# Low parts of projection weights by a negated copy and an adding transfer

## The chip, the cores and the metric

The kernel runs on one core of one Trainium2 chip. The metric is device time in microseconds of one execution. The engines: TensorE (PE) multiplies matrices, VectorE (DVE) and ScalarE (ACT) work elementwise on SBUF and PSUM, GpSimd (POOL) is a fourth, programmable engine, SyncE (SP) issues transfers. Sixteen DMA engines carry all transfers. A transfer can be put on the queue of SP, ACT or POOL.

## The reference

A two-layer decoder trunk over 1024 tokens of width 1024, in float32. Each layer:

```
h = rmsnorm(x, attn_norm)
proj = h @ w_in                # 1024 x 1952, split among four token mixers
y_a = latent attention (4 heads, rotary key)      y_b = gated convolution
y_c = pooling over 2/4/8/16 positions             y_d = windowed attention with sinks
mixed = per-group rmsnorm of (y_a, y_b, y_c, y_d)
x = x + mixed @ w_o
x = x + (silu(gate) * up) @ w_down,  gate, up = split(rmsnorm(x) @ w_gate_up)
```

After both layers comes a last rmsnorm.

## The kernel before

Every large product is made of three products of rounded halves. A float32 operand is split into a high part, rounded to the matmul's float32r format, and a low part, what is left. `mm3` adds high x high, high x low and low x high in PSUM; for the weights W and activations R the order is (Wh, Rh), (Wh, Rl), (Wl, Rh), so that the low part of the weights is wanted by the third matmul of each group. One matmul takes 128 x 128 weights and 128 x 512 activations. The feed-forward products go through a seven-product scheme on 2 x 2 blocks (the names B11, N1, T3 and so on).

Weights come from memory as float32 and are split on the chip. `weights` (L206 to L220) does it for one block: SP loads the raw block, ScalarE writes the high part (L218), VectorE subtracts it from the raw block and writes the low part (L219). Blocks wider than 256 columns take raw, high and low tiles from a pool of 47 tile places of 128 x 1024 (`slots`); narrower ones have buffers of their own (vraw, vhi, vlo). `weights_slots` (L256) does the same for two blocks of 128 x 1024 of the output projection in each layer, L266 and L267. `first_blocks` splits the first three projection blocks of layer 0 by another helper, `split` (L286, L287). `rope_weights` (L222) splits its block at L231 and L232.

So `weights` with wide tiles handles, over both layers, 27 blocks of 1024 columns of w_in and 16 blocks of 768 columns of w_o; with narrow tiles 22 blocks. `expect_layer` lists the wide blocks in the order of their use and `ahead` fetches the next one. Every one-block `project` makes two products of 24 matmuls, one for each half of the tokens; its result is evicted by VectorE (L360, L488). Every output block makes two products of 18 matmuls (`out_part`), evicted at L1087. `ring` holds two blocks' high and low tiles; places that come free go to the end of the queue of free places.

The order of the work is not the program's. `order_engines` reads all instructions, and `arrange` simulates the engines with a table of durations and gives each engine's queue a fixed order by readiness and rank. MOVED is a list of shifts of the ranks, some 3,700 entries. The instructions of each engine, SP's transfers too, are then issued in that fixed order. For a transfer on GpSimd's queue the table has this line, which no instruction of the kernel before uses:

```
            if eng == "POOL":
                v.ns, v.tail = 700, 4200
```

that is, 700 ns in the queue and 4200 ns more until it has landed. GpSimd's queue holds 32 memsets of attention (L1045, zeros in the last block of a tile in `mix_values`), two products at the very end (L433) and four at the start.

Of the kernel before, what the change touches and what calls it, by code (L numbers as in the profile page):

```python
# [14 lines left out]
AF = mybir.ActivationFunctionType  # L15
ALU = mybir.AluOpType
AX = mybir.AxisListType

P = 128
# [96 lines left out]
def trunk_kernel(ctx: ExitStack, tc: tile.TileContext, ins, out):  # L116
    nc = tc.nc
    act, dve, pe, pool, sp = nc.scalar, nc.vector, nc.tensor, nc.gpsimd, nc.sync
# [11 lines left out]
    def rd(ap):  # L130
        return ap.bitcast(F32)
# [74 lines left out]
    def weights(src, n):  # L206
        if n > 2 * P:
            s = F.pair()
            raw = F.ap2(s)
            sp.dma_start(raw[:, :n], src)  # L210
            hi, lo = (R.ap2(i) for i in ring_next())
            F.free_pair(s)
        else:
            raw = wpool.tile([P, 2 * P], F32, name="vraw", tag="vraw")
            sp.dma_start(raw[:, :n], src)
            hi = wpool.tile([P, 2 * P], F32R, name="vhi", tag="vhi")
            lo = wpool.tile([P, 2 * P], F32R, name="vlo", tag="vlo")
        act.copy(hi[:, :n], raw[:, :n])  # L218
        dve.tensor_tensor(out=lo[:, :n], in0=raw[:, :n], in1=rd(hi[:, :n]), op=ALU.subtract)  # L219
        return hi, lo  # L220

# [36 lines left out]
    def weights_slots(src, m, n):  # L258

        s = F.pair()  # L260
        raw = F.ap2(s)
# [5 lines left out]
        dve.tensor_tensor(out=lo, in0=raw[:, : m * n], in1=rd(hi), op=ALU.subtract)  # L267
# [178 lines left out]
    for l in range(L):  # L446
# [313 lines left out]
        for ct in range(2):  # L760
# [18 lines left out]
            else:  # L779
# [7 lines left out]
                out=dst,  # L787
# [1765 lines left out]
```

## Time and profile before

| What | Value |
|---|---|
| time, median of 3 runs | 2052.42 us (2051.62 to 2052.92) |
| profiled execution, span | 2050.3 us |
| what lies around the span (median less span) | 2.1 us |
| TensorE busy | 2034.3 us |
| VectorE busy | 1599.7 us |
| ScalarE busy | 981.9 us |
| GpSimd busy | 7.9 us |

For the profiled execution only its span is recorded, so the median of the runs stands in for its own time. The span is cut into 40 slices of 51 us in the profile's second part. Layer 0's projections run up to about 190 us, its latent attention and output projection to about 400, its feed-forward part to about 1000; layer 1 then repeats this. Matmuls overlap each other: one lasts about 390 ns in the rows and the next starts 227 ns after it, so that "busy" alone doesn't show whether they follow each other as closely as they can. In the rows of waits the columns are the total in us, how many there were, and the longest one. In the groups the columns are busy time and mean duration in ns, then the idle time before them and what ended it. In the rows of time the columns are start, length, engine, line, operation and shapes.

### The profile page before, as it was taken

How to read it: one execution, taken by the hardware profiler on the slowest of the kernel's cores; microseconds unless marked ns; L12 is line 12 of the kernel's file. 1: busy time of each engine (PE TensorE's matmuls, PEld its weight loads, DVE VectorE, ACT ScalarE, POOL GpSimd, SP SyncE). 2: the span in 40 equal slices, each digit the busy share in tenths (PEclk: the TensorE clock that was granted, in tenths of full speed). 3: DMA queues.
4: the chain of work that ended last, by engine and by line, in shares of the span. 5: the costliest groups of instructions: out<-in, count | busy, mean ns of one | idle time of the engine just before them, and what ended most of it. 6: DMA issues, size and time to landing. Idle time of an engine off the chain costs nothing. (4 is left out here: it accounts for less than half of the span.)

```text
span 2050.3 us, 26022 instructions
## 1 busy us (share of the span) xinstructions
PE 2034.3 (99%) x9418; PEld 1675.7 (82%) x9418; DVE 1599.7 (78%) x2742; ACT 981.9 (48%) x1713; POOL 7.9 (0%) x38
## 2 busy tenths in 40 slices
PE   9999999999999999999999999999999999999997
PEld 7887888888878888888888878877888888888887
DVE  7889988998778887556566898889987877876555
ACT  6447666653333335344443576657433333354342
POOL 0000000000000000000000000000000000000000
PEclk9999999999999999999999999999999999999999
DMA  5020223355445547766411102142564544487552
GB/s 182 24 73 21 74 84 111 113 190 176 161 143 186 172 154 232 240 236 221 139 37 44 47 22 93 57 146 101 175 203 151 179 160 146 167 295 242 172 195 86
DMA packets 149249, 289.74 MB, mean 141 GB/s; under 512 B 12672, under 2 KB 72064, under 8 KB 149120
## 3 DMA queue, kind: packets, MB, share of 16 engines
q1 hardware_dynamic: 148976, 288.03, 41.8%
q8 instruction: 74, 1.21, 0.2%
q14 instruction: 55, 0.45, 0.1%
q10 hardware_dynamic: 144, 0.05, 0.0%
HBM read 204.67 MB, written 83.36 MB: 140 GB/s over the span
## 5 line engine op out<-in xcount | busy, mean ns | idle before, releaser
L275 PE MATMUL ps_mm<-u,u 128*128 128x512 f32 (+1 forms) x3376 | 858.6, 389 | 0.3 <-DVE u L287 0.2
L275 PEld LDWEIGHTS ps_mm<-u,u 128*128 128x128 f32 x3376 | 617.0, 188 | 130.0 <-issue 5.9
L275 PE MATMUL ps_s<-u,u 128*128 128x512 f32 x2666 | 686.0, 390 | 2.4 <-DVE u L287 2.3
L275 PEld LDWEIGHTS ps_s<-u,u 128*128 128x128 f32 x2666 | 499.4, 188 | 109.6 <-DVE u L287 3.2
L286 ACT CAST u<-u 128x1024 fp32r<-128x1024 f32 (+2 forms) x385 | 334.7, 891 | 451.9 <-PE ps_mm L275 92.5
L287 DVE TENSOR_TENSOR u<-u,u 128x1024 fp32r<-128x1024 f32 (+2 forms) x385 | 387.6, 1023 | 161.3 <-ACT u L286 134.6
L275 PE MATMUL ps_t<-u,u 128*128 128x512 f32 (+1 forms) x1122 | 287.5, 379 | 1.0 <-DVE u L1642 1.0
L275 PEld LDWEIGHTS ps_t<-u,u 128*128 128x128 f32 x1122 | 203.5, 188 | 42.6 <-issue 1.7
L275 PE MATMUL ps_pv<-u,u 128*128 128x512 f32 x744 | 214.7, 390 | 0.5 <-ACT u L286 0.5
L275 PEld LDWEIGHTS ps_pv<-u,u 128*128 128x128 f32 x744 | 139.4, 188 | 30.4 <-ACT u L286 0.9
L289 ACT ACTIVATE u<-u,par 128x512 fp32r<-128x512 f32 x100 | 69.0, 717 | 40.5 <-DVE u L360 14.0
L1394 ACT ACTIVATE tp<-tp 128x512 f32<-128x512 f32 x84 | 52.8, 631 | 71.5 <-DVE tp L360 71.4
L164 DVE TENSOR_TENSOR u<-u 128x256 f32<-128x256 f32 x176 | 73.4, 421 | 14.9 <-DMA u<-in_w_dn 12.7
L286 ACT CAST u<-ps_t 128x512 fp32r<-128x512 f32 (+3 forms) x128 | 60.9, 501 | 50.2 <-PE ps_t L1036 28.0
L287 DVE TENSOR_TENSOR u<-ps_t,u 128x512 fp32r<-128x512 f32 (+3 forms) x128 | 71.7, 576 | 13.9 <-ACT u L286 12.7
L1262 ACT COPY tn<-ps_s 128x512 f32<-128x512 f32 x64 | 37.4, 584 | 79.5 <-PE ps_s L275 77.3
L290 DVE SCALAR_TENSOR_TENSOR u<-u,par,u 128x512 fp32r<-128x512 f32 x100 | 72.5, 746 | 3.1 <-ACT u L289 3.0
L321 ACT ACTIVATE tn<-u 128x512 f32<-128x512 f32 (+1 forms) x93 | 52.9, 592 | 35.4 <-DVE u L1642 25.7
L1395 DVE TENSOR_TENSOR tp<-tp,u 128x512 f32<-128x512 f32 x84 | 57.2, 686 | 11.8 <-ACT tp L1394 11.6
L219 DVE TENSOR_TENSOR u<-u,u 128x1024 fp32r<-128x1024 f32 (+1 forms) x43 | 48.1, 1119 | 16.0 <-PE ps_mm L275 6.4
L218 ACT CAST u<-u 128x1024 fp32r<-128x1024 f32 (+1 forms) x43 | 41.8, 971 | 39.0 <-DMA u<-in_w_in 26.7
L360 DVE TENSOR_TENSOR tp<-tp,u 128x512 f32<-128x512 f32 x84 | 57.3, 685 | 0.5
(196 smaller groups left out, 2007.3 us busy)
## 6 DMA issues: line engine op xcount, KB each, us to landing
u<-in_w_gu SPq DMA_DIRECT2D x88, 512.0 KB, 3.9
ad<-u SPq DMA_DIRECT2D x154, 256.0 KB, 2.1
u<-ad SPq DMA_DIRECT2D x70, 512.0 KB, 5.0
u<-in_w_dn SPq DMA_DIRECT2D x68, 512.0 KB, 3.7
qd<-u SPq DMA_DIRECT2D x44, 512.0 KB, 3.2
u<-qd SPq DMA_DIRECT2D x32, 512.0 KB, 5.2
u<-in_w_in SPq DMA_DIRECT2D x27, 512.0 KB, 3.5
u<-in_xT SPq DMA_DIRECT2D x32, 256.0 KB, 5.0
```

What stands on the lines that cost most here:

```text
L164: dve.tensor_tensor(out=o, in0=o, in1=u, op=ALU.add)
L218: act.copy(hi[:, :n], raw[:, :n])
L219: dve.tensor_tensor(out=lo[:, :n], in0=raw[:, :n], in1=rd(hi[:, :n]), op=ALU.subtract)
L275: pe.matmul(o, w, r, start=start and k == 0 and i == 0, stop=stop and k == n - 1 and i == 2, skip_group_check=again,)
L286: act.copy(hi, f)
L287: dve.tensor_tensor(out=lo, in0=f, in1=rd(hi), op=ALU.subtract)
L289: act.activation(hi, f, AF.Copy, scale=gain)
L290: dve.scalar_tensor_tensor(out=lo, in0=f, scalar=gain, in1=rd(hi), op0=ALU.mult, op1=ALU.subtract)
L321: act.activation(q, f, AF.Square)
L360: dve.tensor_tensor(out=o, in0=a, in1=b, op=ALU.mult)
L1394: last_silu = act.activation(g, g, AF.Silu)
L1395: dve.tensor_tensor(out=g, in0=g, in1=r, op=ALU.mult)
```

## The change

For the 47 wide blocks (43 in `weights`, 4 in `weights_slots`) the subtraction on VectorE is gone. ScalarE, after it has written the high part, writes the raw block once more, rounded in the same way and multiplied by -1, into the low tile. A transfer on GpSimd's queue then adds the raw block, read as float32, onto the low tile. What stands in the low tile is again raw less rounded. The 22 narrow blocks, `first_blocks` and `rope_weights` are as before. The list MOVED is replaced by another one (3,776 entries for 3,708), so the order of all engines' instructions is another one as well; the functions that make the order are the same.

```diff
         act.copy(hi[:, :n], raw[:, :n])
-        dve.tensor_tensor(out=lo[:, :n], in0=raw[:, :n], in1=rd(hi[:, :n]), op=ALU.subtract)
+        if n > 2 * P:
+            rest(lo[:, :n], raw[:, :n])
+        else:
+            dve.tensor_tensor(out=lo[:, :n], in0=raw[:, :n], in1=rd(hi[:, :n]), op=ALU.subtract)
         return hi, lo
+
+    def rest(lo, raw):
+
+        act.activation(lo, raw, AF.Copy, scale=-1.0)
+        pool.dma_start(rd(lo), raw, accum_op=ALU.add)
...
         act.copy(hi, raw[:, : m * n])
-        dve.tensor_tensor(out=lo, in0=raw[:, : m * n], in1=rd(hi), op=ALU.subtract)
+        rest(lo, raw[:, : m * n])
         return h, l
...
 MOVED = """
...
 """
```

704 rows, old and new, of the table MOVED are left out of this document.

## The prediction

> **What bounds the kernel now.** I read the page first: engine shares and the slices.
>
> ```profile
> span 2050.3 us, 26022 instructions
> PE 2034.3 (99%) x9418; PEld 1675.7 (82%) x9418; DVE 1599.7 (78%) x2742; ACT 981.9 (48%) x1713; POOL 7.9 (0%) x38
> PE   9999999999999999999999999999999999999997
> DVE  7889988998778887556566898889987877876555
> PE 27%; DVE 0%; ACT 0%; issue 0%; DVEq 0%
> ```
>
> TensorE is busy in all 40 slices but the last, and the chain that ended last is nearly all TensorE. VectorE, which the change relieves, is 78% busy and has two humps: slices 3 to 9 and 23 to 29. A busy TensorE could still hide short stalls, so I compare its pace. Then the stages:
>
> ```profile
> 1825.55 22.44 PE ps_s L275 x99
> ...
> 0.00:25.00 25.00, 23.83 (x101) 19.33 (x102) 19.46 (x35) 20.20 (x32) 0.20 (x4) 1.00 0.88 320
> 25.00:190.00 165.00, 165.00 (x805) 135.85 (x804) 134.57 (x294) 92.50 (x204) 0.00 (x0) 1.00 0.13 43
> 190.00:350.00 160.00, 159.17 (x807) 129.97 (x805) 141.57 (x306) 105.70 (x245) 3.26 (x16) 1.00 0.23 75
> ...
> 450.00:1000.00 550.00, 548.28 (x2419) 453.47 (x2418) 407.50 (x587) 219.03 (x292) 0.00 (x0) 1.00 0.57 192
> 1000.00:1200.00 200.00, 200.00 (x960) 164.70 (x959) 139.16 (x296) 93.42 (x203) 0.00 (x0) 1.00 0.15 48
> 1200.00:1350.00 150.00, 149.51 (x751) 121.53 (x750) 133.48 (x290) 98.66 (x228) 2.65 (x14) 1.00 0.21 69
> 2000.00:2050.00 50.00, 39.86 (x296) 37.37 (x294) 28.20 (x57) 14.42 (x33) 1.41 (x2) 0.94 0.24 85
> ```
>
> Columns: window, length, busy time of TensorE, its weight loads, VectorE, ScalarE, GpSimd, granted clock, DMA share, GB/s. In the chain 99 matmuls take 22.44 us, 226.7 ns each; 2419 of them make 548.4 us of the 550 in the feed-forward stage, so that stage runs at the matmul's own pace. TensorE's idle time is 16.0 us over the span: 10.1 in the last 50 us, 1.2 in the first 25, 1.7 in the feed-forward, and 1.3 in the two stages 190 to 350 and 1200 to 1350, where the layers' attention runs and VectorE is 88% and 89% busy (141.57/160, 133.48/150). The changed weights are made between 25 and 350 and between 990 and 1360. The waits say what little TensorE waited for:
>
> ```profile
> PE ps_s L275 <- DVE u L287: 2.3, 2, 1.7
> PE ps_mm L275 <- DVE u L913: 1.3, 4, 0.6
> PE ps_mm L275 <- DVE u L287: 0.2, 1, 0.2
> ...
> PEld ps_s L275 <- DVE u L287: 3.2, 2, 2.2
> PEld ps_t L1036 <- DVE u L287: 2.2, 10, 0.3
> PEld ps_mm L275 <- DVE u L287: 0.9, 2, 0.7
> PEld ps_pv L1048 <- DVE u L287: 0.9, 5, 0.2
> PEld ps_mm L848 <- DVE u L360: 0.7, 2, 0.4
> PEld ps_mm L275 <- DVE u L219: 0.6, 2, 0.4
> ```
>
> TensorE's matmuls waited 3.8 us for VectorE (first three rows), its weight loads at least 8.5 us (the last six, which contain the first three's stalls in part). For the subtraction that goes away, L219, weight loads waited 0.6 us.
>
> **The change, part by part.** Prices:
>
> ```profile
> L219 DVE TENSOR_TENSOR u<-u,u 128x1024 fp32r<-128x1024 f32 x27 | 32.9, 1220 | 15.2 <-PE ps_mm L275 6.4 <-PE ps_pv L340 3.7 <-PE ps_t L275 2.9
> L219 DVE TENSOR_TENSOR u<-u,u 128x768 fp32r<-128x768 f32 x16 | 15.2, 950 | 0.7 <-ACT u L218 0.6
> L267 DVE TENSOR_TENSOR u<-u,u 128x1024 fp32r<-128x1024 f32 x4 | 4.9, 1221 | 0.8 <-ACT u L266 0.8
> L728 ACT ACTIVATE u<-u,par 128x1024 f32<-128x1024 f32 x4 | 4.6, 1144 | 3.5 <-DVE u L360 3.5
> L1021 ACT ACTIVATE u<-u,sm 128x512 f32<-128x512 f32 x16 | 10.9, 721 | 1.6 <-DVE sm L1016 1.6
> ...
> qd<-u SPq DMA_DIRECT2D x44, 512.0 KB, 3.2
> u<-qd SPq DMA_DIRECT2D x32, 512.0 KB, 5.2
> ```
>
> Removed: 47 subtractions, 32.9 + 15.2 + 4.9 = 53.0 us of VectorE, which falls to 1546.7 us (75%). The 22 narrow blocks and the first three blocks of layer 0 keep theirs.
>
> Added on ScalarE: 47 scaled copies. A scaled copy of 1024 columns is the L728 row, 1.14 us; 768 columns by the line through L728 and L1021 are 0.93 us. 31 x 1.14 + 16 x 0.93 = 50.3 us; ScalarE goes to 1032 us, 50%. In 190 to 350 it gets some 2 x 1.14 more for the joint blocks, 1.14 for the last projection block and 8 x 0.93, 11 us on 105.7 of 160, 73%: it doesn't become the bound there. Its cover is that idle quarter; without it the 11 us would stand ahead of the splits (L286) that matmuls wait for.
>
> Added on GpSimd's queue: 47 transfers of 512 or 384 KB within the SBUF, in a queue that held only memsets in these stages. The trace has no adding transfer and none issued by GpSimd. Below: the plain 512 KB store, 3.2 us. Above: the addition reads two streams, so twice the plain load, 10.4 us. I take 5, by the single load (5.2) and by what the kernel's own order writer plans (700 ns of issue and 4200 to landing), for which the new order was written. Engines for it are free: DMA shares are 0.13 to 0.23 in these stages; 47 times 3.2 to 10.4 us of all 16 engines is 150 to 490 us beside 2050. Memsets wait behind it for its issue, by the plan 0.7 us: the 32 memsets are hidden as long as a block's other matmuls cover that; without cover at most 20 transfers in attention x 0.7 = 14 us.
>
> What gets later is the low part: before, 1.22 us behind the rounded part, now 1.14 + 5, so 4.9 us later at the same place in the order (2 us at 3.2, 10.3 at 10.4). The raw tile is held as long, and loads that take its place start later. What covers this is the distance from the low part to its first matmul:
>
> ```profile
> 1054.76 1.23 DVE L219 TENSOR_TENSOR u<-u,u 128x1024 fp32r<-128x1024 f32 x1 [2.05 <-PE ps_t L275]
> 1103.13 0.69 DVE L488 SCALAR_TENSOR_TENSOR te<-ps_mm,u 128x512 f32<-128x512 f32 x1 [0.32 <-PE ps_mm L275]
> ...
> 342.10 0.96 DVE L219 TENSOR_TENSOR u<-u,u 128x768 fp32r<-128x768 f32 x1 [0.19 <-ACT u L218]
> 362.78 0.68 DVE L1087 TENSOR_TENSOR u<-u,ps_mm 128x512 f32<-128x512 f32 x1
> ...
> 86.07 1.22 DVE L219 TENSOR_TENSOR u<-u,u 128x1024 fp32r<-128x1024 f32 x1
> 95.94 0.69 DVE L360 TENSOR_TENSOR u<-ps_mm,u 128x512 f32<-128x512 f32 x1 [1.82 <-PE ps_mm L275]
> 260.63 0.95 DVE L219 TENSOR_TENSOR u<-u,u 128x768 fp32r<-128x768 f32 x1
> 267.14 0.69 DVE L1087 TENSOR_TENSOR u<-u,ps_mm 128x512 f32<-128x512 f32 x1 [0.52 <-PE ps_mm L275]
> 1273.24 0.95 DVE L219 TENSOR_TENSOR u<-u,u 128x768 fp32r<-128x768 f32 x1
> 1281.17 0.69 DVE L1087 TENSOR_TENSOR u<-u,ps_mm 128x512 f32<-128x512 f32 x1 [0.82 <-PE ps_mm L275]
> ```
>
> Each pair is a low part and the eviction of its first product, matched by counting both in program order. From an eviction I go back 24 matmuls (5.4 us; 18 and 4.1 for the output projection); where the eviction shows a wait for TensorE it follows the product at once, in the second pair it may stand later, so that its cover is an upper bound. Layer 1's seventh block is ready at 1056.0 and used by 1097.7: 42 us of cover. The last output block of layer 0 has 343.1 to 358.7, 16 us. The shortest: layer 0's fifth streamed block (87.3 to 90.5, 3 us) and the third output block of both layers (261.6 to 263.0, 1.5 us, and 1274.2 to 1277.1, 2.9 us). So 4.9 us more is hidden nearly everywhere by work already ahead; at the three places it would cost 1.9 + 3.4 + 2.0 = 7.3 us if the order stayed. The new order counts on 4.9 us, so I take 0 for it and keep 7.3 for the range.
>
> Two notes from outside the sum. The Trainium skill ("DMA: Bandwidth & Descriptors", Anatomy of one DMA) gives a GpSimd transfer some 2.0 us plus bytes at 436 GB/s, by my estimate 3.2 us for 512 KB without addition; with that the low part would be 3 us later and the second place would cost 1.6 us, the third 0.2; no row of this profile shows such a transfer. Against the change stands "SBUF — State Buffer" (the "DVE blocks DMA" trap): GpSimd can't write its descriptors while VectorE runs an operation that uses both ports. What would do that here are the rescalings of attention:
>
> ```profile
> 78.27 1.15 DVE L609 TENSOR_SCALAR tp<-tp,sm 128x256 f32<-128x256 f32 x4
> ```
>
> Four in a row hold VectorE 1.15 us, so a transfer issued at such a moment lands 1.15 us later.
>
> The sum: VectorE's relief gives back some of the 3.8 us of matmul waits. The removed work lies only partly ahead of them: in 190 to 350 it is about 11 of 141.57 us, which brings that stage from 88% to 81%. I take half, 1.9 us. Late low parts 0, ScalarE 0, memsets 0. 2050.3 - 1.9 = 2048.4 of span. The median of the runs is 2052.42, 2.1 above the span, so 2050.5.
>
> **The rivals.**
>
> More comes back. Beyond the visible gaps lie the weight loads' 8.5 us: if VectorE's humps are what keeps the order tight, the new order can pack TensorE closer there. For: 88 and 89% busy. Against: 10.1 us of the idle time lie at the end, where nothing changes. Up to 8.5, likeliest 7: 2045.
>
> The low parts come late (slower). Place: third output block of each layer and the fifth streamed block. It decides once low parts come more than 1.5 us later than now; at 4.9 us and unmoved matmuls 7.3 us, 2050.5 + 7.3 = 2058. For: third block's raw load ends right ahead of its rounding, so nothing can be made earlier there. Against: 13 us and more of cover elsewhere, and an order that plans for it.
>
> The addition takes 10.4 us. Then low parts are 10.3 us later: 7.3 + 8.8 + 7.4 = 23.5 us at these places, 2074.
>
> GpSimd held up by VectorE's rescalings: 1.15 at each of three places, 3.5 us: 2054. I give it little, since rescalings are 4 in a row at most and the covers are long.
>
> Nothing of VectorE's 53 us was on the path: 2052.4. The change would do what it says and show it only in VectorE's share.
>
> **How the numbers follow.** Forecast (2047 to 2054) 0.42; more comes back 0.28; late low parts 0.14; slow addition 0.07; rescalings 0.03; nothing 0.06. About 0.2%, 4.1 us, is what a measurement can tell from no change: faster is below 2048.3, slower above 2056.5. Faster: 0.28 + 0.06 of the forecast's lower edge = 0.34. Slower: 0.14 + 0.07 + 0.01 = 0.22. The rest, 0.44, is the same. The range takes in 2052.4 - 8.5 and some rounding of it, 2042, and late low parts with half again their price, 2062; outside stay the slow addition and the extremes, about 0.13.
>
> **What would show it.** VectorE near 1547 us and ScalarE near 1032; 47 scaled copies of 0.93 to 1.14 us; 47 transfers of GpSimd landing in about 5 us. TensorE still at 99% with 10 us idle at the end. The forecast is wrong if weight loads wait more than a few us for GpSimd's transfers, above all around 263 and 1277, or if TensorE's idle time in 190 to 350 changes by more than a few us; a landing time above 7 us would point to the late cases.

## The result, and the profile after

The changed kernel takes 2101.07 us (median of 4 runs, 2099.52 to 2107.25), the kernel before beside it 2052.33 (2051.62 to 2052.92): a ratio of 1.0242, 95% interval 1.0227 to 1.0257. It is 48.7 us slower. The profiled execution has a span of 2100.7 us, 50.4 more than before. From the page of the changed kernel:

```profile
span 2100.7 us, 26162 instructions
PE 2054.7 (98%) x9418; PEld 1672.6 (80%) x9418; DVE 1554.9 (74%) x2695; ACT 1021.6 (49%) x1760; POOL 48.2 (2%) x85
PE   9999899999999999999999999999999999999998
DVE  6778786988778777655646897779987687775645
PE 80%; DVE 7%; DMA 7%; ACT 3%; issue 2%; SPq 0%; DVEq 0%; ACTq 0%; POOLq 0%
```

VectorE lost 44.8 us of work and ScalarE gained 39.7, where the prediction had 53.0 and 50.3. TensorE falls below 9 only in slice 5, at about 210 to 260 us, and in the last. The chain that ended last passes through VectorE, transfers and ScalarE for 17% of the span. That can't be set against the zeros of the page before: there the chain could be followed back over the last 27% of the span only. What was added has these prices (groups by shape, then transfers with their size and the median time from issue to landing):

```profile
L227 ACT ACTIVATE u<-u 128x1024 fp32r<-128x1024 f32 x31 | 32.8, 1058 | 12.7 <-DMA u<-in_w_in 5.8 <-DVE sm L368 3.1 <-PE ps_mm L283 2.0
L227 ACT ACTIVATE u<-u 128x768 fp32r<-128x768 f32 x16 | 13.5, 847 | 5.4 <-DMA u<-in_w_o 4.7 <-DVE u L298 0.5
L228 POOL DMA_DIRECT2D u<-u x47 | 40.7, 867 | 1238.1 <-ACT u L227 1131.0 <-ACT u L294 38.7 <-PE ps_s L583 21.6
```

```profile
u<-u POOLq DMA_DIRECT2D x31, 512.0 KB, 4.8
u<-u POOLq DMA_DIRECT2D x16, 384.0 KB, 4.5
```

In the mean nothing costs more than was thought: copies of 1.06 and 0.85 us, transfers that land after 4.8 and 4.5 us (medians; the 47 lie between 3.9 and 7.8). The stages, with the columns of the prediction's table:

```profile
190.00:350.00 160.00, 152.22 (x743) 121.83 (x742) 126.33 (x282) 108.41 (x245) 10.24 (x23) 0.97 0.35 92
450.00:1000.00 550.00, 543.11 (x2372) 443.28 (x2372) 400.74 (x586) 205.79 (x273) 0.00 (x0) 1.00 0.56 187
1000.00:1200.00 200.00, 197.99 (x952) 164.86 (x951) 123.97 (x270) 102.79 (x204) 10.38 (x12) 1.00 0.41 110
1200.00:1350.00 150.00, 146.26 (x701) 116.01 (x699) 122.27 (x255) 102.38 (x216) 8.64 (x18) 1.00 0.31 80
```

In 190 to 350 TensorE issues 743 matmuls where it had issued 807, and in 1200 to 1350 it issues 701 for 751. So far this fits late low parts. The feed-forward row doesn't: 2372 for 2419, though no changed weight and no adding transfer runs there (GpSimd: 0.00). What TensorE's matmuls waited for in the changed kernel (total, times, longest):

```profile
PE ps_s L283 <- DVE te L1585: 6.9, 3, 4.4
PE ps_t L283 <- ACT u L294: 3.8, 3, 2.0
PE ps_s L283 <- DVE u L295: 3.3, 2, 2.8
PE ps_mm L283 <- DMA u<-u: 2.9, 2, 1.9
```

For the adding transfers themselves (`DMA u<-u`) its matmuls waited 2.9 us and its weight loads 3.7. The waits are spread over many lines, most of which the change's code doesn't touch. The changed part that does touch them is the list of shifts, which sets the order of every engine.

### The profile page after: what moved, and what is told of

It reads as the page before. It is cut to its first block, busy times and chain, and to the rows that moved or that the text cites. A ratio compares the mean times of both kernels' runs of the same rounds, so it can differ in the third digit from the quotient of the medians.

```text
span 2100.7 us, 26162 instructions
## 1 busy us (share of the span) xinstructions
PE 2054.7 (98%) x9418; PEld 1672.6 (80%) x9418; DVE 1554.9 (74%) x2695; ACT 1021.6 (49%) x1760; POOL 48.2 (2%) x85
## 4 chain that ended last, share of the span: by engine, by line
PE 80%; DVE 7%; DMA 7%; ACT 3%; issue 2%; SPq 0%; DVEq 0%; ACTq 0%; POOLq 0%
PE ps_mm L283 30%; PE ps_s L283 24%; PE ps_t L283 10%; PE ps_pv L283 7%; DVE u L295 2%; DMA u<-in_w_o 2%; PE ps_pv L1056 1%; PE ps_t L1044 1%; DMA ad<-u 1%; ACT u L294 1%; PE ps_t L353 1%; DMA u<-in_w_in 1%; DMA u<-in_w_dn 1%; DMA u<-in_w_gu 1%; PE ps_s L991 1%
## 5 line engine op out<-in xcount | busy, mean ns | idle before, releaser
L283 PE MATMUL ps_s<-u,u 128*128 128x512 f32 x2666 | 676.5, 392 | 13.3 <-DVE te L1585 6.9
L283 PE MATMUL ps_pv<-u,u 128*128 128x512 f32 x744 | 208.4, 391 | 1.4 <-ACT u L294 1.3
L228 POOL DMA_DIRECT2D u<-u x47 | 40.7, 867 | 1238.1 <-ACT u L227 1131.0
```

The lines of the kernel that those rows point to most:

```text
L228: pool.dma_start(rd(lo), raw, accum_op=ALU.add)
L283: pe.matmul(o, w, r, start=start and k == 0 and i == 0, stop=stop and k == n - 1 and i == 2, skip_group_check=again,)
```

## Experiments: order or transfers

Two theories. "Order": the new issue order is worse on the chip, transfers or not. "Transfers": the later low parts, longer held raw tiles and added traffic cost the time. The first pair crosses the two parts of the change. The issue order of one kernel is written out step by step and given to the other kernel's code:

```diff
-    for queue in arrange(steps).values():
+    for part in np.split(ranks, np.cumsum(ORDER_N)[:-1]):   # ranks: the other kernel's order
+        queue = [steps[r] for r in np.cumsum(part)]
```

The new order with VectorE's subtractions:

> The changed kernel's issue order on every engine, written out step by step, but each of the 47 low parts is again one VectorE subtraction, at the place of the negated copy (or right behind the rounding, where the copy stood ahead of it); no adding transfer runs. Theory 'order' (the new list of shifts gives an order that fits late loads badly; the adding transfers themselves cost little): 2085 to 2105 us, as slow as the change. Rival 'transfers' (the later low parts, the longer held raw tiles or the traffic of the adding transfers delay the loads and TensorE): 2050 to 2062 us.

Measured: 2103.97 us (ratio 1.0247, 1.0229 to 1.0265). Without a single adding transfer the new order is as slow as the change. It is not a pure test, since 53 us of VectorE's work are back in an order that has no room for them.

The old order with the new low parts:

> The kernel before's issue order on every engine, written out step by step; in place of each of the 47 subtractions stands, at the same moment of that order, the negated copy on ScalarE's queue and the adding transfer on GpSimd's. Theory 'order': 2048 to 2062 us (2052.4 plus at most the 7.3 us that late low parts were to cost at three places, less up to 4 for VectorE's relief). Rival 'transfers': 2085 us and more, since every load and low part is delayed as in the changed kernel, with an order that does not plan for it.

Measured: 2146.92 us (1.0458, 1.0442 to 1.0473), 94 us slower than before. Here "order" missed: the adding transfers are very expensive when the order isn't made for them. TensorE's waits in this kernel, the first rows:

```profile
PE ps_mm L285 <- DMA u<-u: 47.7, 14, 6.0
PE ps_mm L285 <- DVE u L923: 5.5, 2, 4.7
PE ps_t L355 <- DVE u L336: 4.9, 3, 1.7
PE ps_s L993 <- ACT u L296: 3.4, 1, 3.4
```

So both parts can cost, each alone. The list of shifts can also be emptied in both kernels:

```diff
-MOVED = """ ... """
+MOVED = ""
```

> The kernel before with an empty list of shifts, so that its order follows the planner's own priorities. Its order writer puts the end at 2067.8 us instead of 2039.9. Both theories: 2075 to 2120 us. It is the pair of after_plain.

> The changed kernel with an empty list of shifts; the order writer puts the end at 2076.3 us, 8.6 more than for before_plain. Theory 'order': within 15 us of before_plain, since neither has a list of shifts. Rival 'transfers': 35 to 60 us more than before_plain, as between the two kernels.

Measured: 2085.48 us (1.0157, 1.0140 to 1.0174) and 2101.83 us (1.0238, 1.0218 to 1.0259). Without lists the new low parts cost 16.4 us, just above the 15 that "order" allowed and far from the 35 to 60 of "transfers". The kernel before gains 33 us from its list. The changed kernel gains nothing measurable from its own (2101.83 without, 2101.07 with), though its order writer promised 32 us (2076.3 to 2044.0).

## Experiments: the order without the addition

To keep VectorE relieved and yet take away everything that the transfers bring, the addition alone is left out (the low parts are then incomplete):

```diff
         act.activation(lo, raw, AF.Copy, scale=-1.0)
-        pool.dma_start(rd(lo), raw, accum_op=ALU.add)
```

In the new order:

> The changed kernel in its own issue order with the 47 adding transfers left out: the low parts hold only the negated rounding, so the output is not the reference's; they are ready right behind the copy, the raw tiles come free at once, and GpSimd's queue moves nothing. VectorE is relieved as in the change. Theory 'order': 2088 to 2102 us, within about 10 us of the changed kernel's 2101. Rival 'transfers': 2045 to 2065 us, since everything that the transfers bring is gone.

Measured: 2086.68 us (1.0164, 1.0150 to 1.0178). That lies between the theories, just under what "order" expected. Of the 48.7 us, 33.9 stay when nothing lands late and no transfer is added; 14.4 go with the transfers (2101.07 less 2086.68; each run's own runs of the kernel before differ by a few tenths, so the two don't add up exactly). The two rows of stages that matter:

```profile
190.00:350.00 160.00, 157.71 (x789) 126.84 (x788) 129.33 (x289) 113.10 (x252) 2.84 (x16) 1.00 0.23 73
450.00:1000.00 550.00, 542.95 (x2363) 442.60 (x2362) 396.25 (x573) 208.22 (x277) 0.00 (x0) 0.99 0.56 188
```

The transfers' share shows in attention (789 matmuls here, 743 with the addition, 807 before). The feed-forward stage is as slow as with the addition (2363 and 2372), so its loss isn't the transfers'.

In the old order:

> The kernel before's issue order with each subtraction replaced by the negated copy at the same moment, and no adding transfer (low parts incomplete, output not the reference's). What is left of the change is 47 more copies on ScalarE, at the place of the subtractions, and VectorE's relief. If the 94 us that the full change cost in this order are the landing time of the transfers: 2050 to 2062 us. If ScalarE's copies, which hold back what stands behind them in its queue, are a large part: above 2080 us.

Measured: 2058.43 us (1.0025, 1.0016 to 1.0035). Of the 94 us that the full change costs in the old order, 88.5 are the transfers; 5.7 are left for 47 more copies in ScalarE's queue, less whatever VectorE's relief gave back. The two runs without the addition hold the same code in two orders, and 28.3 us lie between them (2086.68 and 2058.43): that much is the order's alone, with this code. The 33.9 us hold the copies too.

## Experiments: cover

Why 88 us? I went through the trace of before again and followed each of the 47 low parts to the first matmul that reads it, by the program's own dependencies instead of by its eviction. Thirteen have less than 4.9 us of cover, not three. Three pairs that the prediction had missed, a low part on VectorE and the first matmul that needs it, in the kernel before:

```profile
205.61 1.23 DVE L219 TENSOR_TENSOR u<-u,u 128x1024 fp32r<-128x1024 f32 x1
206.93 1.39 PE L275 MATMUL ps_mm<-u,u 128*128 128x512 f32 x5
...
1308.84 0.95 DVE L219 TENSOR_TENSOR u<-u,u 128x768 fp32r<-128x768 f32 x1
1310.13 0.94 PE L275 MATMUL ps_mm<-u,u 128*128 128x512 f32 x3
...
1344.19 0.96 DVE L219 TENSOR_TENSOR u<-u,u 128x768 fp32r<-128x768 f32 x1 [0.43 <-ACT u L218]
1345.20 2.12 PE L275 MATMUL ps_mm<-u,u 128*128 128x512 f32 x8
```

The low parts end at 206.84, 1309.79 and 1345.15; covers of 0.1, 0.3 and 0.05 us. Over the thirteen, 4.9 us less the cover adds up to 46.8 us, beside the 47.7 us that TensorE waited for `DMA u<-u` in old_order_new_lows. Thirteen of the fourteen waits there stand at exactly these matmuls; the fourteenth is 0.3 us long. If cover decides, the 47 blocks split in two: those with long cover and no load waiting for their raw tile (25, by the order writer's times), and the rest:

```diff
+        if block in ON_VECTOR:      # 22 blocks in hidden_only, the other 25 in exposed_only
+            dve.tensor_tensor(out=lo, in0=raw, in1=rd(hi), op=ALU.subtract)
+            return
         act.activation(lo, raw, AF.Copy, scale=-1.0)
         pool.dma_start(rd(lo), raw, accum_op=ALU.add)
```

> The kernel before's issue order; 25 of the 47 low parts by negated copy and adding transfer, those whose first use lies so far behind, and whose raw tile is wanted so late, that 4.9 us fit in between by the order writer's own times; the other 22 stay VectorE subtractions. 'Cover decides' (a transfer costs what its landing outlasts the cover): 2048 to 2056 us. If each transfer costs something by traffic or by holding a queue: 94 x 25/47 = 50 us more than before, about 2100.

> The complement: the kernel before's issue order, adding transfers for the other 22 low parts only (short cover, or a raw tile that the next load is waiting for), VectorE for the 25. 'Cover decides': 2135 to 2150 us, nearly all of the 94 us. If each transfer costs alike: 2052.5 + 94 x 22/47 = 2097 us.

Measured: hidden_only 2052.63 us (0.9999, 0.9990 to 1.0008), exposed_only 2145.46 us (1.0447, 1.0433 to 1.0461). Twenty-five adding transfers cost nothing that can be measured (the interval is some 2 us either way), the other twenty-two cost 93 us, nearly all that the 47 cost together. So the transfers don't cost alike, by traffic or by their place in GpSimd's queue. And relieving VectorE of 25 subtractions, net of 25 copies on ScalarE, shows no gain either. TensorE's first row of waits in exposed_only:

```profile
PE ps_mm L291 <- DMA u<-u: 47.5, 13, 5.8
```

Thirteen waits of 47.5 us stand against a loss of 93, so something comes on top of them. One of them in old_order_new_lows, in order of time (start, length, what ran, and in brackets the wait ahead of it):

```profile
1271.20 4.06 PE L285 MATMUL ps_mm<-u,u 128*128 128x512 f32 x17
...
1273.72 1.04 ACT L229 ACTIVATE u<-u 128x1024 fp32r<-128x1024 f32 x1
1275.12 0.86 POOL L230 DMA_DIRECT2D u<-u  x1 [19.81 <-ACT u L229]
...
1279.69 6.58 PE L285 MATMUL ps_mm<-u,u 128*128 128x512 f32 x17 [4.42 <-DMA u<-u]
```

Seventeen matmuls take 4.06 us ahead of the wait and 6.58 behind it. The same stretch of that kernel in windows of 2 us (TensorE's count stands in the first brackets, the granted clock third from the end):

```profile
1276.00:1278.00 2.00, 0.00 (x0) 0.00 (x0) 1.80 (x3) 0.00 (x0) 0.00 (x0) 1.00 0.85 164
1278.00:1280.00 2.00, 0.31 (x1) 0.32 (x2) 0.00 (x0) 0.27 (x1) 0.00 (x0) 0.52 0.53 98
1280.00:1282.00 2.00, 2.00 (x6) 1.52 (x6) 1.41 (x2) 2.00 (x4) 0.00 (x0) 0.50 0.00 0
1282.00:1284.00 2.00, 2.00 (x6) 1.61 (x5) 1.25 (x2) 2.00 (x6) 0.00 (x0) 0.50 0.00 0
1284.00:1286.00 2.00, 2.00 (x8) 1.55 (x8) 1.89 (x3) 0.14 (x2) 0.00 (x0) 0.77 0.00 0
1286.00:1288.00 2.00, 2.00 (x11) 1.62 (x10) 0.00 (x0) 0.00 (x0) 0.35 (x2) 1.00 0.51 137
```

After an idle gap of 4.4 us the clock is 0.50 to about 1285, and TensorE issues 6 matmuls in 2 us where it issues 11 once the clock is back.

The Trainium skill ("TensorE: Matmul & The Clock Gate", Part 1: The HAM clock gate) says that one idle window of some 3.4 us halves TensorE's clock and that about as long a busy stretch restores it. This trace agrees on the half clock (0.50); here some 5 us of work went by before it was restored, and elsewhere in this run a gap of 3.0 us was enough.

How much of the 94 us is this? Old_order_new_lows and the kernel before issue the same 9418 matmuls in the same order, so the two traces can be laid side by side, matmul by matmul. The last matmul starts 94.3 us later than before. Of this, 50.1 us arise at the 14 waits for adding transfers, 24.1 at 140 matmuls that ran at the reduced clock, 19.3 at waits for VectorE and ScalarE, and 0.8 elsewhere. All but some 2 us of it arises between 164 and 418 and between 1134 and 1380 us (times of the kernel before); in the feed-forward stages the lateness stays as it is. The waits for VectorE and ScalarE have in the main a second cause:

```profile
245.58 0.37 ACT L921 CAST u<-ps_mm 128x256 fp32r<-128x256 f32 x1 [4.04 <-DMA u<-u]
...
246.77 0.42 DVE L923 TENSOR_TENSOR u<-ps_mm,u 128x256 fp32r<-128x256 f32 x1 [4.02 <-ACT u L921]
...
248.53 0.55 PE L285 MATMUL ps_mm<-vhi,u 128*128 128x256 f32 x1 [4.71 <-DVE u L923]
```

The cast at L921 reads no low part. By the program, the tile place that it writes is the one of the raw block which the adding transfer issued at 241.13 was still reading. ScalarE waits for an adding transfer in this way nine times for over 2 us, 38 us in all, each time for the place of a raw block. So a transfer costs in two ways: its low part comes late, and its raw tile is held. In hidden_only neither TensorE nor ScalarE waits for an adding transfer at all.

## Experiments: what is wrong with the new order

New_order_no_add left 33.9 us without any transfer, 28.3 of them the order's. Both orders come from a table of durations. The kernel before runs 10 us longer than its order writer says (2039.9, span 2050.3), the changed kernel 57 us longer (2044.0, span 2100.7). SyncE's transfers of both kernels, issue to landing; first before, then after:

```profile
u<-in_w_gu SPq DMA_DIRECT2D x88, 512.0 KB, 3.9
u<-in_w_o SPq DMA_DIRECT2D x16, 384.0 KB, 3.1
```

```profile
u<-in_w_gu SPq DMA_DIRECT2D x88, 512.0 KB, 4.0
u<-in_w_o SPq DMA_DIRECT2D x16, 384.0 KB, 4.0
```

The feed-forward loads land alike, so the new order isn't slow because transfers got much slower there. It may be slow because it can't bear the ones that land late, which both kernels have: beside the order writer's times the median transfer of SyncE is 0.28 us late before and 0.35 after, one in twenty over 2.2 and 2.6. As a calculation, not a run: with each trace's own landing times in the order writer's model, its end moves by 5 us for the kernel before and by some 36 for the changed one. The test on the chip gives the order writer an allowance for every transfer of SyncE's queue (2000 with the lists, 2500 without):

```diff
-                v.end = wire + 345 if v.stores else wire + 470 + v.size / 1885.0
+                v.end = wire + 345 + 2000 if v.stores else wire + 470 + 2000 + v.size / 1885.0
```

> The changed kernel with an empty list of shifts (its pair is after_plain, 2101.8 us), and an order writer that counts on 2.5 us more for every transfer of SyncE's queue. Its own end stays at 2075.5 us (2076.3 without the allowance). If the orders of the change lose their time because transfers land later than the order writer thinks: 2078 to 2090 us. If late landings aren't the cause: 2098 to 2106, as after_plain.

> The changed kernel with its own list of shifts and 2.0 us more for every transfer of SyncE's queue in the order writer. The writer's own end gets worse, from 2044.0 to 2065.4 us, since the list was made for the other landing times. Late landings the cause: faster than the change all the same, 2075 to 2095 us. Not the cause: 2101 plus 21 us, about 2120.

> The kernel before with the same allowance of 2.0 us; the writer's end goes from 2039.9 to 2071.8 us. If its list holds on the chip as it is (10 us between the writer's end and the span): slower than before, 2075 to 2090 us. If an allowance helps any order: below 2052 us.

Measured: after_plain_loads2500 2085.59 us (1.0157, 1.0142 to 1.0172), after_loads2000 2090.59 (1.0184, 1.0167 to 1.0201), before_loads2000 2091.35 (1.0183, 1.0168 to 1.0199). With the allowance the changed kernel is 16 us faster without a list and 10.5 us faster with its own, although for the latter the writer's own end, by its old table, became 21 us worse. The kernel before loses 38 us, a little more than I expected: its list already fits the chip as it is, and another table unfits it. One stage of after_plain, then of after_plain_loads2500:

```profile
1200.00:1350.00 150.00, 142.72 (x660) 112.13 (x659) 116.68 (x239) 95.45 (x200) 7.79 (x17) 0.97 0.30 79
```

```profile
1200.00:1350.00 150.00, 144.46 (x684) 115.38 (x683) 121.20 (x250) 100.63 (x216) 8.02 (x17) 0.99 0.30 81
```

Twenty-four more matmuls in the same 150 us, by a plan that assumes worse transfers. So landings that are later than planned seem to be a part of the order's loss, 10 to 16 us by these runs. An allowance also changes the order in other ways, and that late landings are all of the 28 us is not shown: why the rest of the order is slower stays open.

The last run asked whether an order fitted anew could use VectorE's freed time. It starts from hidden_only and changes only places in its written-out queues, by a search against the order writer's model:

```diff
-ORDER = (... hidden_only's queues ...)
+ORDER = (... the same queues, some 40 small moves ...)
```

> hidden_only (25 covered low parts by negated copy and adding transfer, 22 on VectorE), its order moved step by step, some 40 small moves, so that the order writer's own times, with loads that land up to 3.5 us late, end earlier (2054.4 us on the mean of six such draws instead of about 2056). If the VectorE time that hidden_only frees (25 subtractions, 30 us) is worth something once the order is fitted to it: 2044 to 2050 us, faster than the kernel before. If VectorE's time wasn't on the path: 2050 to 2054, the same.

Measured: 2058.78 us (1.0029, 1.0018 to 1.0041), slower than the 2052.63 it started from. Neither expectation holds. The model that the moves were chosen by promised a gain of 1 to 2 us and the chip lost 6. It is the same on a small scale as the change's own list, with 32 us promised and none delivered. No version here beats the kernel before.

## Why the prediction was wrong

The forecast was 2050.5 us, the range 2042 to 2062, and the measured time is 2101.07.

Prices: right or near. VectorE was to fall to 1546.7 us and fell to 1554.9; ScalarE was to reach 1032 and reached 1021.6; the copies were to take 0.93 to 1.14 us and took 0.85 and 1.06; the transfers were to land in 5 us and land in 4.5 to 4.8, three of the 47 after more than 7. The rival of a slow addition (10.4 us) is out by these rows.

Readings that were wrong: the chain that ended last ("nearly all TensorE") covers 27% of the span, from 1482 us on, and says nothing about the stages with the changed weights. At a landing time of 3.2 us the low part comes 3.1 us later (1.14 + 3.2 - 1.22), not "2 us" as in the brackets.

VectorE's relief, 1.9 us: not found. Hidden_only takes 26.5 us of work from VectorE (1573.2 for 1599.7) and leaves the time where it was, to 0.2 us, with an interval of some 2 us either way and 25 copies more on ScalarE. The waits for VectorE that I wanted to halve belonged to other instructions than the subtractions.

ScalarE at nothing: not quite. In the old order the copies, net of VectorE's relief, cost 5.7 us. A quarter of idle time over a stage didn't hide copies that stand ahead of others in a queue.

Cover, the first step that failed: "at the three places it would cost 1.9 + 3.4 + 2.0 = 7.3 us". The mechanism was right; the count was wrong, and a held raw tile had no price. I went back from evictions by a fixed number of matmuls, wrote down the shortest I saw, and took the rest as covered ("13 us and more"). There are thirteen such places, worth 46.8 us by the same formula and 47.7 us by measurement. The three that I had are among them, but the third block of layer 1 has 1.15 us of cover to its first matmul, where I counted 2.9. The half-speed clock after the gaps (24 us) and the waits behind held raw tiles and other late results (19 us) come on top: 94 us in the old order, where my rival of late low parts said 7.3. The half-speed clock was in no term of my sum.

"The new order counts on 4.9 us, so I take 0 for it", the second and larger one. I took an order that plans for the landing time as being as good as the old one. In it the transfers still cost 14.4 us, and 33.9 more stay without them, 28.3 by the order alone and some 6 by the copies, if they cost there what they cost in the old order. I had priced the code of the change and given the replaced list no term at all; its only trace in my sum was that zero. The profile of before could have warned of this: a kernel with 16 us of TensorE's idle time in 2050 has an order that fits the chip closely, and another list can lose that (33 us, by the empty one).

The signs named in advance held in part. TensorE's idle time in 190 to 350 went from 0.8 to 7.8 us, as in "wrong if". At 1277 weight loads were to wait for GpSimd's transfers, but over the whole run they waited for those for 3.7 us only, at 213 and 1294; the rest of the loss stood in rows I had not thought to watch, the feed-forward stage above all.

GpSimd held up by VectorE's rescalings was not tried in a run. The trace of the changed kernel shows no sign of it where the two meet:

```profile
1121.31 0.86 POOL L228 DMA_DIRECT2D u<-u  x1 [21.65 <-PE ps_s L583]
1121.31 0.34 DVE L617 TENSOR_SCALAR tp<-tp,sm 128x256 f32<-128x256 f32 x1
1122.17 0.61 DVE L617 TENSOR_SCALAR tp<-tp,sm 128x256 f32<-128x256 f32 x2
```

One rescaling ran beside this transfer's issue and two more right behind it. The issue took 0.86 us as the others do, and the transfer landed 4.55 us after it, below the median of its size. What the delay of memsets behind the transfers costs was not tried.

## What to carry to other kernels

A replaced schedule is a change of its own, with its own price: cross it with the code (old order with new code, new order with old code, neither list) before believing anything about the code. Price a later operand at every place that reads it, by the dependency and not by a sample, price the tile that is held for it as well, and add the slow clock behind each gap of TensorE (1.0 to 2.8 us for each gap of 3 us or more in old_order_new_lows). An order that looks better only in its own table of durations may be worse on the chip; the one to trust is the one whose plan and trace agree.

## What the runs showed of the hardware

In old_order_new_lows each of the twelve TensorE gaps of 3.0 to 6.0 us brought 3.4 or 6.8 us of granted clock at 0.50; the gaps of 1.9 us and less did not. In the changed kernel three gaps of 1.9 to 2.3 us did, while two of 2.8 us did not. After the gap of 4.4 us shown above, 17 matmuls took 6.58 us for 4.06. An adding transfer of 512 KB within the SBUF lands 4.8 us (median) after its issue on GpSimd's queue, within the range of the loads of that size by SyncE in the same trace (medians of 3.8 to 5.2 us), and 25 adding transfers beside a full TensorE cost nothing that can be measured.
